# Two left sides of the fast products begin 192 bytes further, and four small tiles get four buffers: a four-layer hybrid trunk

## Chip, cores and metric

One core of one Trainium2 chip runs the whole program. The metric is the device time of one execution in microseconds; a kernel's figure is the median of its runs. The engines are named as in the profile: PE (TensorE matmul), PEld (its weight loads), DVE (VectorE), ACT (ScalarE), POOL (GpSimd), SP (the queue that issues most transfers).

## What is computed

A trunk of four layers over x of 512 rows by 1024 columns, all float32. Each layer adds a mixer's output and then a feed-forward network's output to x:

```python
for layer in range(4):
    h = rmsnorm(x, norm_mix[layer])
    mix = s5_mixer / gla_mixer / diff_attn_mixer / s5_mixer   # layers 0, 1, 2, 3
    x = x + mix
    h = rmsnorm(x, norm_ffn[layer])
    g, u = split(h @ w_gate_up)          # 1024 x 5632
    x = x + (silu(g) * u) @ w_down       # 2816 x 1024
return rmsnorm(x, norm_final)
```

The mixers are a diagonal state-space scan (S5, layers 0 and 3), gated linear attention (GLA, layer 1) and differential attention with a chunk mask (layer 2).

## The kernel before

**Number format.** A float32 factor is split into a high half (rounded to fp32r) and a low half (the rest). ACT writes the high half with a cast, DVE the low half with a subtraction. A product is then three fp32r matmuls: high by high, high by low, low by high. Weights are staged from memory into "wst" or "slot" tiles and split into "whl" tiles, which have five buffers (methods `high` and `low`, lines 366 and 374).

**The feed-forward product in seven products.** The product with `w_gate_up` is done per block of 256 hidden columns, 11 blocks in each layer. In a block the four quarter products of rows and depth are replaced by seven products of sums of quarters, a scheme with seven multiplications in place of eight. Each of the seven takes a left side (256 rows by 512 of depth of the normed input, or a sum of such quarters) and a right side (512 by 256 of the weights, or a sum). The left sides are made once in a layer and are used by all 11 blocks. There are seven:

- "11" and "12" lie in one tile, `sides`, of the activations' room (the pool `hp`, tag `hT`, two buffers). That room also holds the normed activations of the mixers and the tile `halves`, from which all left sides are made. `Sides.room` takes both tiles.
- "1", "2", "4", "3" and "22" are tiles `side...` of the layer's own pool `ffn0` to `ffn3`, taken by `Sides.open`. Two small tiles named `edge` (64 and 192 bytes) stand among these to set where they begin.

One product is `seven_product`, whose matmuls all have line 561: two column halves, four depth tiles and three terms, that is 24 matmuls of 128x128 by 128x256. The right side's piece is the stationary operand, loaded by PEld; the left side's piece, 256 columns of float32, is the moving operand:

```python
mm(o, hl[:, x, k, c], side[:, y, k], start=..., stop=...)
```

The PSUM bank's name tells the products apart in the profile: "one" (bank a, sides), "five" (bank c, side), "six" (a, side), "two" (d, sides), "seven" (a, side), "three" (c, side), "four" (a, side), which is also the order of the third and later blocks. So in a block the first "a" and the "d" read `sides`, the five others a `side` tile. Each layer's first two blocks are instead interleaved step by step by a plan that is written out by hand in `ffn`; it holds the making of the left sides ("total", "high", "low") as well, and the "six" of the first block needs the sum that `add22a`, `highSa` and `lowSa` make of two weight quarters. After each three or four blocks come the matmuls of the down projection (lines 394 to 396, whl as moving operand).

**Where the tiles begin.** Pools lie one behind the other in each partition: constants, x, the activations' room `hp`, weights and staging `wp`, norm tiles `normp`, statistics `small`, and then the pool of the stage at work (`ffn0` and so on). By the sizes of the tiles the two buffers of `hp` begin at bytes 30,656 and 47,040, both 192 past a multiple of 256. The five side tiles begin at 132,736 and further, all 128 past a multiple of 256 (and in layers 0 and 3 three of them 384 past a multiple of 512, all others 128).

**Statistics tiles.** The pool `small` gives each kind eight buffers where nothing else is said, and each buffer takes at least 32 bytes. Four kinds matter here: `ms2` (GLA's `readout`, one for each of eight readouts), `st` (one for each of eight heads of the differential attention), `sums` (one for each of its 32 score steps) and `nm` (two for each score step: the row maximum, written by DVE at line 2261 and read by the exponential on ACT at line 2265). The probabilities `pr` of the score steps have four buffers, two for a step.

**Order of the work.** In GLA and the differential attention the order on PE is the written one, and the framework's planner orders the other engines; in the plan of the feed-forward layers all engines follow the written order; in the later blocks the planner orders all of them. Waits come from the planner.

Of the kernel before, what the change touches and what calls it, by code (L numbers as in the profile page):

```python
# [11 lines left out]
F32 = mybir.dt.float32  # L12
F32R = mybir.dt.float32r
# [8 lines left out]
P = 128  # L22
D = 1024
SEQ = 512
NT = SEQ // P
# [42 lines left out]
class Left:  # L68
# [18 lines left out]
    def room(self):  # L87
        self.hT = [self.tr.hp.tile([P, KT, SEQ], F32R, tag="hT", name=f"hT{z}") for z in range(2)]
# [72 lines left out]
class Sides(Left):  # L161
# [13 lines left out]
    def room(self):  # L175
        F = self.tr.hp.tile([P, 4, 4, 256], F32, tag="hT", name="halves")
        self.whole = F
        self.F = {(0, 0): F[:, 0], (1, 0): F[:, 1], (0, 1): F[:, 2], (1, 1): F[:, 3]}
        two = self.tr.hp.tile([P, 2, 2, 4, 256], F32R, tag="hT", name="sides")
        self.place = {"11": two[:, 0], "12": two[:, 1]}  # L180
        self.heads = []

# [104 lines left out]
class Trunk:  # L287
# [278 lines left out]
    def seven_block(self, fp, slots, left, wgu, b, turn, na):  # L566
# [48 lines left out]
        def room1(room=None):  # L615
            load("1", 0, 1, (0, 0), room)

        def room22(room=None):
            load("22", 1, 1, None, room)
# [93 lines left out]
    def ffn(self, l, left, after=None, turn=False, aside=None, small=None):  # L713
# [7 lines left out]
        with self.tc.tile_pool(name=f"ffn{l}", bufs=1, reuse_waits="tile") as fp:  # L721
# [6 lines left out]
            if glued:  # L728
                lent = room()
# [1123 lines left out]
    def gla(self, l, left):  # L1853
# [5 lines left out]
        with self.tc.tile_pool(name="gla", bufs=1) as p:  # L1859
# [32 lines left out]
            hT = left.hT  # L1892
# [79 lines left out]
            def readout(hf, t):  # L1972
                st, o_h = sts[hf], on[hf]
                oo = row(self.tp("op"))
                ms = self.sp.tile([P, 2], F32, tag="ms2", name="ms")
                for z in range(2):
                    h = 2 * hf + z
                    zs = slice(z * 256, (z + 1) * 256)
                    for c in range(2):
                        ch = 2 * t + c  # L1980
                        nc.tensor.matmul(
                            oo[c * 64 : (c + 1) * 64, zs], qT[:, h, ch * 64 : (ch + 1) * 64], st[z][:, ch],
                            start=True, stop=True,
                        )
                for z in range(2):
                    junk = T("e")
                    nc.scalar.activation(
                        junk[:, :256], oo[:, z * 256 : (z + 1) * 256], AF.Square, scale=1.0 / 16.0,
                        accum_out=ms[:, z : z + 1],
                    )  # L1990
                r_ = self.rsqrt(ms[:], 2, 1e-6)
                for z in range(2):
                    h = 2 * hf + z
                    zs = slice(z * 256, (z + 1) * 256)
                    v.scalar_tensor_tensor(
                        o_h[:, t, zs], oo[:, zs], r_[:, z : z + 1], ng[:, h * 256 : (h + 1) * 256],
                        op0=ALU.mult, op1=ALU.mult,
                    )
# [25 lines left out]
            def core(hf):  # L2024


                def after0():
                    if hf:
                        readout(0, 3)
                    updates(hf, 0)  # L2030

                def after1():
                    readout(hf, 0)
                    updates(hf, 1)

                def after2():
                    readout(hf, 1)
                    updates(hf, 2)

                def after3():  # L2040
                    readout(hf, 2)
                    updates(hf, 3)

                return after0, after1, after2, after3
# [84 lines left out]
    def diff(self, l, left):  # L2129
# [4 lines left out]
        with self.tc.tile_pool(name="diff", bufs=1) as p:  # L2134
# [6 lines left out]
            hT, r = left.hT, left.r  # L2141
# [83 lines left out]
            def prepare(j):  # L2225


                room, bufs, tag = (self.wp, 5, "whl") if j == 1 else (p, 1, "hl")
                hl = room.tile([P, 2, 2, SEQ], F32R, tag=tag, name="hl", bufs=bufs)
                src = qks[j // 4][:, :, j % 4]  # L2230
                nc.scalar.copy(hl[:, 0], src)
                v.tensor_tensor(hl[:, 1], src, hl[:, 0].bitcast(F32), op=ALU.subtract)
                qs = p.tile([P, 2, SEQ], F32R, tag="qs", name="qs", bufs=2)
                ks = self.wp.tile([P, 2, 2, SEQ], F32R, tag="whl", name="ks", bufs=5)
                for m in range(2):
                    rows = slice(m * 64, (m + 1) * 64)
                    for z in range(2):
                        to = slice(z * 64, (z + 1) * 64)
                        self.nc.gpsimd.dma_start(qs[to, m], hl[rows, z, 0])
                        self.nc.gpsimd.dma_start(ks[to, m], hl[rows, :, 1])  # L2240
                ready[j] = qs, ks
                st = self.sp.tile([P, 2, NT], F32, tag="st", name="st")
                o_s = p.tile([P, NT, P], F32, tag="o_s", name="o_s", bufs=2)
                kept[j] = st, o_s

# [2 lines left out]
            def scores(i):  # L2248
                j, t = divmod(i, NT)
                ts = slice(t * P, (t + 1) * P)  # L2250
                qs, ks = ready[j]
                st = kept[j][0]
                pr, sums = [], self.sp.tile([P, 4], F32, tag="sums", name="sums")
                ss = [self.sbank("s"), self.sbank("s")]
                for m in range(2):
                    for z in range(2):
                        nc.tensor.matmul(ss[m][:], qs[:, m, ts], ks[:, m, z], start=z == 0, stop=z == 1)  # L2257
                for m in range(2):
                    e = T("pr", 4)
                    nm = self.sp.tile([P, 1], F32, tag="nm", name="nm")  # L2260
                    v.tensor_tensor_reduce(  # L2261
                        e[:], ss[m][:], mask[:, t], -0.125, 3e38, op0=ALU.add, op1=ALU.min, accum_out=nm[:]
                    )
                    sum_ = st[:, 0, t : t + 1] if m == 0 else sums[:, 1:2]
                    nc.scalar.activation(e[:], e[:], AF.Exp, scale=-1.0, bias=nm[:], accum_out=sum_)  # L2265
                    pr.append(e)
                v.reciprocal(sums[:, 2:3], sums[:, 1:2])
                v.tensor_scalar(
                    sums[:, 3:4], st[:, 0, t : t + 1], sums[:, 2:3], self.neglam[:], op0=ALU.mult, op1=ALU.mult
                )  # L2270
                a = pr[0]
                v.scalar_tensor_tensor(a[:], pr[1][:], sums[:, 3:4], pr[0][:], op0=ALU.mult, op1=ALU.add)
                soft[i] = a
# [52 lines left out]
            run(units, 8)  # L2326
            rest()
            prepare(0)
            run(units)

# [17 lines left out]
            done, w1 = {}, []  # L2348
            run(units, 2)
            scores(0)  # L2350
            run(units, 6)
            scores(1)
            run(units, 2)
            for i in range(32):
                j, t = divmod(i, NT)
                if i == 15:
                    run(units)
                    rest()
                src, n = (units, (3, 3)) if i < 15 else (last, (1, 1))
                if i in (15, 28, 31):  # L2360
                    n = (0, 0)
                elif i == 29:
                    n = (0, 2)
                aT = turned(i)
                if t == 0 and j < 7:
                    prepare(j + 1)
                if i < 30:
                    scores(i + 2)
                if i in done:
                    done.pop(i)()  # L2370
                run(src, n[0])
                values(i, aT)
                run(src, n[1])
                if i in (16, 31):
                    back(i // 31)
                if i in (26, 29):
                    w1 += [self.wb(wo, kb, 512) for kb in ((0, 2) if i == 26 else (4, 6))]
                if t == 3:
                    done[i + (2 if j in (6, 7) else 3)] = normalised(j)
# [96 lines left out]
```

## Time and profile before

| | |
|---|---|
| median of three runs | 2313.63 us (2310.96 to 2320.4) |
| the profiled execution | 2315.56 us, of which the span from first to last instruction is 2313.8 |
| mean granted PE clock | 0.987 |
| busy: PE, DVE, ACT, POOL | 2223.6, 1570.6, 1120.3, 280.8 us |
| transfers | 317.83 MB, mean 137 GB/s |
| feed-forward layers (seven products and down projections) | about 243 to 587, 832 to 1139, 1455 to 1764, 1962 to 2268 us |

How to read it: busy time of PE is counted from the start of a matmul to its modelled end, and matmuls overlap, so 24 matmuls of some 280 ns each follow each other in under 3 us. The chain of waits lists, in order of time, the pieces of work that the end of the program waited for: start, length, engine, bank or tile, line and count. In the groups of instructions "out<-in" gives tile names without buffer numbers, and the figure behind the bar is the sum of busy time, then the mean duration.

### The profile page before, as it was taken

How to read it: one execution, taken by the hardware profiler on the slowest of the kernel's cores; microseconds unless marked ns; L12 is line 12 of the kernel's file. 1: busy time of each engine (PE TensorE's matmuls, PEld its weight loads, DVE VectorE, ACT ScalarE, POOL GpSimd, SP SyncE). 2: the span in 40 equal slices, each digit the busy share in tenths (PEclk: the TensorE clock that was granted, in tenths of full speed). 3: DMA queues.
4: the chain of work that ended last, by engine and by line, in shares of the span. 5: the costliest groups of instructions: out<-in, count | busy, mean ns of one | idle time of the engine just before them, and what ended most of it. 6: DMA issues, size and time to landing. Idle time of an engine off the chain costs nothing. (4 is left out here: it accounts for less than half of the span.)

```text
span 2313.8 us, 37222 instructions
## 1 busy us (share of the span) xinstructions
PE 2223.6 (96%) x14847; PEld 1970.8 (85%) x14847; DVE 1570.6 (68%) x2430; ACT 1120.3 (48%) x1865; POOL 280.8 (12%) x386
## 2 busy tenths in 40 slices
PE   5889999999999999999999999999999899999997
PEld 3778979898877799998987787999999788989996
DVE  7873887776624468777744675876766864967674
ACT  5624645454452456555535675744534224635342
POOL 1000141513000011101002131110000100101000
PEclk8999999999999999999999999999999999999999
DMA  4246667664322357666336465886641546766531
GB/s 86 40 112 182 141 165 181 156 176 117 112 73 78 124 134 197 182 164 174 99 116 146 92 143 149 208 225 151 157 109 46 141 142 163 181 166 165 157 79 64
DMA packets 295320, 317.83 MB, mean 137 GB/s; under 512 B 72206, under 2 KB 235338, under 8 KB 294891
## 3 DMA queue, kind: packets, MB, share of 16 engines
q1 hardware_dynamic: 232906, 234.23, 34.0%
q0 software_dynamic: 62240, 81.22, 19.0%
q8 instruction: 117, 1.92, 0.3%
q14 instruction: 57, 0.46, 0.1%
HBM read 283.54 MB, written 16.65 MB: 130 GB/s over the span
## 5 line engine op out<-in xcount | busy, mean ns | idle before, releaser
L374 DVE TENSOR_TENSOR whl<-wst,whl 128x1024 fp32r<-128x1024 f32 x272 | 331.6, 1224 | 256.2 <-ACT whl L366 255.6
L366 ACT CAST whl<-wst 128x1024 fp32r<-128x1024 f32 x272 | 283.9, 1050 | 314.5 <-PE acc L396 223.7
L561 PE MATMUL a<-side,whl 128*128 128x256 f32 x3168 | 385.6, 278 | 6.1 <-ACT r L633 4.3
L561 PEld LDWEIGHTS a<-side,whl 128*128 128x128 f32 x3168 | 373.3, 189 | 7.8 <-ACT r L633 5.1
L394 PE MATMUL acc<-whl,act 128*128 128x512 f32 x704 | 278.3, 396 | 0.9 <-DVE x L544 0.9
L395 PE MATMUL acc<-whl,act 128*128 128x512 f32 x704 | 274.7, 390 | 0.0
L396 PE MATMUL acc<-whl,act 128*128 128x512 f32 x704 | 274.7, 390 | 0.0
L561 PE MATMUL c<-side,whl 128*128 128x256 f32 x2112 | 254.1, 277 | 1.2 <-DVE whl L374 1.2
L561 PEld LDWEIGHTS c<-side,whl 128*128 128x128 f32 x2112 | 246.7, 188 | 1.8 <-DVE whl L374 1.8
L374 DVE TENSOR_TENSOR whl<-slot,whl 128x1024 fp32r<-128x1024 f32 x107 | 130.5, 1223 | 69.6 <-ACT whl L366 69.6
L394 PEld LDWEIGHTS acc<-whl,act 128*128 128x128 f32 x704 | 132.1, 188 | 31.3 <-issue 2.3
L396 PEld LDWEIGHTS acc<-whl,act 128*128 128x128 f32 x704 | 132.2, 188 | 28.1
L395 PEld LDWEIGHTS acc<-whl,act 128*128 128x128 f32 x704 | 132.2, 188 | 25.6
L366 ACT CAST whl<-slot 128x1024 fp32r<-128x1024 f32 x107 | 112.3, 1054 | 81.9 <-PE acc L396 35.1
L394 PE MATMUL acc<-whl,hT 128*128 128x512 f32 x352 | 143.3, 407 | 2.3 <-DVE ro L2203 1.5
L395 PE MATMUL acc<-whl,hT 128*128 128x512 f32 x352 | 138.4, 393 | 0.9 <-DVE whl L374 0.9
L396 PE MATMUL acc<-whl,hT 128*128 128x512 f32 x352 | 138.4, 393 | 0.0
L561 PE MATMUL d<-sides,whl 128*128 128x256 f32 x1056 | 133.7, 283 | 3.2 <-ACT whl L366 3.2
L561 PE MATMUL a<-sides,whl 128*128 128x256 f32 x1056 | 134.4, 283 | 0.0
L561 PEld LDWEIGHTS d<-sides,whl 128*128 128x128 f32 x1056 | 129.0, 191 | 4.0 <-ACT whl L366 4.0
L561 PEld LDWEIGHTS a<-sides,whl 128*128 128x128 f32 x1056 | 129.7, 191 | 1.1
L700 ACT CAST act<-r 128x512 fp32r<-128x512 f32 (+1 forms) x110 | 66.2, 644 | 113.3 <-DVE r L679 105.2
(452 smaller groups left out, 3897.8 us busy)
## 6 DMA issues: line engine op xcount, KB each, us to landing
wst<-in_ffn_w_gate_up_dram SPq DMA_DIRECT2D x88, 512.0 KB, 4.7
wst<-in_ffn_w_down_dram SPq DMA_DIRECT2D x88, 512.0 KB, 4.2
slot<-in_ffn_w_gate_up_dram SPq DMA_DIRECT2D x71, 512.0 KB, 6.2
wst<-in_ffn_w_gate_up_dram POOLq DMA_DIRECT2D x44, 512.0 KB, 6.1
halves<-in_ffn_w_gate_up_dram SPq DMA_DIRECT2D x43, 512.0 KB, 5.8
wst<-in_s_w_glu_dram SPq DMA_DIRECT2D x32, 512.0 KB, 4.8
wst<-in_gla_w_in_dram SPq DMA_DIRECT2D x24, 512.0 KB, 3.8
wst<-in_diff_w_qkv_dram SPq DMA_DIRECT2D x24, 512.0 KB, 3.7
```

Of the source, the lines that this page charges most:

```text
L366: self.last["high"] = self.nc.scalar.copy(hl[:, 0], w[:])
L374: self.last["low"] = self.nc.vector.tensor_tensor(hl[:, 1], w[:], hl[:, 0].bitcast(F32), op=ALU.subtract)
L394: mm(out, lh, rh, start=first, stop=False)
L395: mm(out, lh, rl, start=False, stop=False)
L396: self.last["mm"] = mm(out, ll, rh, start=False, stop=last)
L561: mm(o, hl[:, x, k, c], side[:, y, k], start=first and not (j or k or n), stop=k == 3 and n == 2, skip_group_check=True,)
L700: self.last["act high"] = nc.scalar.copy(dst[:, 0, j], src[:, j])
```

## The change

The tile of "11" and "12" becomes a tile of 4160 float32 per partition (16,640 bytes) of which 4096 are used, from the 48th on, that is 192 bytes further. With it each of the two buffers of the activations' room becomes 256 bytes larger, for all tiles that share the tag. The second buffer then begins 256 bytes further (47,296), the pools behind it 512. The two possible places of the sides are 30,848 and 47,488, 128 past a multiple of 256.

The kinds `ms2`, `st`, `sums` and `nm` get four buffers in place of eight, 16 buffers of 32 bytes fewer, 512 bytes. The pools of the stages then begin where they did.

```diff
         F = self.tr.hp.tile([P, 4, 4, 256], F32, tag="hT", name="halves")
...
-        two = self.tr.hp.tile([P, 2, 2, 4, 256], F32R, tag="hT", name="sides")
+        two = self.tr.hp.tile([P, 4160], F32R, tag="hT", name="sides")
+        two = two[:, 48:4144].rearrange("p (s z k n) -> p s z k n", s=2, z=2, k=4)
         self.place = {"11": two[:, 0], "12": two[:, 1]}
...
-                ms = self.sp.tile([P, 2], F32, tag="ms2", name="ms")
+                ms = self.sp.tile([P, 2], F32, tag="ms2", name="ms", bufs=4)
...
-                st = self.sp.tile([P, 2, NT], F32, tag="st", name="st")
+                st = self.sp.tile([P, 2, NT], F32, tag="st", name="st", bufs=4)
...
-                pr, sums = [], self.sp.tile([P, 4], F32, tag="sums", name="sums")
+                pr, sums = [], self.sp.tile([P, 4], F32, tag="sums", name="sums", bufs=4)
...
-                    nm = self.sp.tile([P, 1], F32, tag="nm", name="nm")
+                    nm = self.sp.tile([P, 1], F32, tag="nm", name="nm", bufs=4)
```

## The prediction

> **What bounds the kernel now.** I read the page first, then the busy time by stretches for the four feed-forward layers, then the chain of waits through one of them, then the tiles' own rows.
>
> ```profile
> PE 2223.6 (96%) x14847; PEld 1970.8 (85%) x14847; DVE 1570.6 (68%) x2430; ACT 1120.3 (48%) x1865; POOL 280.8 (12%) x386
> ...
> L561 PE MATMUL a<-side,whl 128*128 128x256 f32 x3168 | 385.6, 278 | 6.1 <-ACT r L633 4.3
> ...
> L561 PE MATMUL c<-side,whl 128*128 128x256 f32 x2112 | 254.1, 277 | 1.2 <-DVE whl L374 1.2
> ...
> L561 PE MATMUL d<-sides,whl 128*128 128x256 f32 x1056 | 133.7, 283 | 3.2 <-ACT whl L366 3.2
> ...
> L561 PE MATMUL a<-sides,whl 128*128 128x256 f32 x1056 | 134.4, 283 | 0.0
> ```
>
> The same line, the same shape, the same right side (whl): a matmul whose moving operand is one of the five "side" tiles takes 277 to 278 ns, and one whose moving operand lies in the "sides" tile of the activations' room takes 283. Nothing of this is clock or luck, as the spread shows (minimum/median/maximum):
>
> ```profile
> L561 PE MATMUL a<-sides,whl x1056: 274/283/387, 243.1 to 2251.2; 128*128 128x256 f32 x176
> L561 PE MATMUL d<-sides,whl x1056: 274/283/388, 249.4 to 2259.5; 128*128 128x256 f32 x176
> ...
> L561 PE MATMUL a<-side,whl x3168: 276/276/580, 260.6 to 2267.7; 128*128 128x256 f32 x198
> L561 PE MATMUL c<-side,whl x2112: 276/276/387, 255.1 to 2265.0; 128*128 128x256 f32 x192
> ```
>
> A duration here covers a pipeline's depth; what counts is start to start. The chain of waits (start, length, what) gives it, in layer 2's steady blocks:
>
> ```profile
> 1584.60 2.87 PE a L561 x24
> 1587.47 2.74 PE c L561 x24
> 1590.21 2.72 PE a L561 x24
> 1592.93 2.86 PE d L561 x24
> 1595.79 2.74 PE a L561 x24
> 1598.53 2.72 PE c L561 x24
> ...
> 1612.29 2.86 PE d L561 x24
> ```
>
> The first "a" of a block (product "one") and the "d" (product "two") read sides; they take 2.86 to 2.87 us for 24 matmuls (119 ns each). A product on a side tile takes 2.72 (113 ns), but 2.74 when it follows a sides product. From one "d" to the next is 1612.29 - 1592.93 = 19.36 us: seven products, no gap, TensorE alone on the chain. And it is so nearly everywhere in the feed-forward layers:
>
> ```profile
> 243.00:587.00 344.00, 341.30 (x2746) 309.68 (x2745) 266.73 (x409) 174.91 (x292) 98.76 (x148) 1.00 0.59 151
> 832.00:1139.00 307.00, 303.87 (x2251) 287.39 (x2250) 243.67 (x364) 171.63 (x244) 33.83 (x35) 1.00 0.60 157
> 1455.00:1764.00 309.00, 305.84 (x2251) 289.43 (x2250) 231.05 (x267) 154.44 (x207) 28.21 (x24) 0.99 0.64 162
> 1962.00:2268.00 306.00, 303.56 (x2251) 287.75 (x2250) 219.83 (x244) 145.70 (x187) 24.24 (x19) 1.00 0.56 143
> ```
>
> Columns: stretch, its length, then busy PE, PEld, DVE, ACT, POOL. Of each layer's 306 to 344 us TensorE is idle 2.4 to 3.2.
>
> **The change, part by part.**
>
> *The sides tile begins 192 bytes further.* By the allocation of the kernel, the five side tiles begin 128 bytes past a multiple of 256 in all layers (in layers 0 and 3 three of them 384 past a multiple of 512), the sides tile 192 past. The change puts it at 128. The trace shows no other difference between the two kinds than this and the room they lie in, so I take the side tiles' price: a block's seven products would take 7 x 2.72 = 19.04 us in place of 19.36, that is 0.32 per block and 0.16 per sides product (0.14 its own, 0.02 the follower's). Two in each of 11 blocks in 4 layers are 88 products, 14.1 us in all. Bounds from the rows for one product: 0 (no change of rate) and 0.16; a better rate than 2.72 no row shows.
>
> Not all of it arrives. At the start of each layer two blocks are interleaved by a written plan, and there VectorE sets the pace (stretches from the start of that to the third block in layers 0 and 3, and layer 2's steady blocks for contrast; VectorE is the third busy figure):
>
> ```profile
> 248.00:291.00 43.00, 41.71 (x357) 41.10 (x356) 39.63 (x48) 27.39 (x36) 7.62 (x9) 1.00 0.55 126
> ...
> 1967.60:2010.50 42.90, 41.51 (x356) 40.99 (x354) 39.63 (x48) 27.29 (x36) 6.25 (x5) 1.00 0.71 179
> 1584.40:1661.90 77.50, 77.50 (x674) 77.46 (x674) 61.10 (x72) 42.88 (x58) 7.69 (x6) 1.00 0.69 171
> ```
>
> 39.63 of 43 us is 92%, against 61.10 of 77.50, 79%. Where TensorE meets that pace, in layer 0 (DVE's and PE's timelines; start, length):
>
> ```profile
> 259.57 1.22 DVE L374 TENSOR_TENSOR whl<-lent,whl 128x1024 fp32r<-128x1024 f32 x1 [0.53 <-ACT whl L366]
> ...
> 260.60 3.03 PE L561 MATMUL a<-side,whl 128*128 128x256 f32 x24
> ...
> 287.33 2.78 PE L561 MATMUL c<-side,whl 128*128 128x256 f32 x22 [0.40 <-DVE whl L374]
> 291.23 0.50 PE L561 MATMUL a<-side,whl 128*128 128x256 f32 x2 [1.11 <-ACT r L633]
> 292.66 0.39 PE L561 MATMUL d<-sides,whl 128*128 128x256 f32 x1 [0.93 <-ACT whl L366]
> ```
>
> Product "six" of the first block starts at 260.60 with its low right half done at 259.57 + 1.22 = 260.79: there is no slack. The four sides products before it (one and two of both blocks) would bring TensorE there 0.64 us sooner, to wait for the same VectorE result; I count them at nothing. The 43 us between go at VectorE's pace, and the third block's "one" is followed by waits of 0.40, 1.11 and 0.93 for ACT and VectorE: its 0.16 is lost too. Five of 22 are absorbed per layer. The third block's "two" and all later ones run without a wait: 17 per layer.
>
> In layer 2 more is lost, since there the chain leaves TensorE for a transfer:
>
> ```profile
> 1509.96 2.63 PE d L561 x22
> ...
> 1513.66 10.13 DMA wst<-in_ffn_w_gate_up_dram
> ...
> 1532.29 3.09 PE a L561 x24
> ```
>
> The "two" at 1509.96 still counts, the fourth block's two sides products (between 1513.66 and 1532.29) are waited away behind that load. So 3 x 17 + 15 = 66 products x 0.16 = 10.6 us.
>
> Wait and clock: TensorE's clock drops after those waits, in some layers.
>
> ```profile
> 293.58:297.00 3.42, 3.42 (x19) 3.42 (x17) 3.42 (x4) 1.44 (x2) 0.00 (x0) 0.50 0.02 5
> 880.68:884.09 3.41, 2.48 (x21) 2.29 (x20) 3.41 (x5) 3.41 (x5) 0.00 (x0) 1.00 1.23 192
> 1505.32:1508.73 3.41, 2.89 (x13) 2.90 (x14) 3.41 (x6) 2.79 (x5) 1.02 (x1) 0.50 1.11 335
> 2010.49:2013.90 3.41, 2.34 (x17) 2.14 (x18) 3.41 (x5) 3.41 (x6) 0.80 (x1) 1.00 0.45 74
> ```
>
> The figure before the last two is the granted clock: 0.50 for 3.41 us in layers 0 and 2, 1.00 at the same place in 1 and 3. One costs at most 3.41 x 0.5 = 1.7 us. The change lengthens the idle time there by 0.16 in some 2.5, so the two may become one, three or none: 3.4 us to either side, taken as no change. The Trainium skill (TensorE: Matmul & The Clock Gate, "What's actually happening") calls the window a free-running one of 3413 ns; the rows agree in length, and in that equal places differ.
>
> *Room behind it moves.* The activations' buffers grow by 256 bytes each, so weights, staging and norm tiles lie 512 further, the second activations' buffer 256 further; each keeps its place within 256. No instruction, transfer or queue entry is added or moved. Cost nothing; its upper bound is the rival below.
>
> *Four buffers in place of eight* for ms2, st, sums, nm. This frees 16 x 32 = 512 bytes, so the layers' pools start where they did. Sixteen more tiles reuse a buffer (four of each kind) and may need a semaphore entry each; the chain shows such entries as pieces of this size:
>
> ```profile
> 1994.30 0.04 issue
> ...
> L2265 ACT ACTIVATE pr<-pr,nm x64: 705/722/732, 1249.9 to 1418.8; 128x512 f32<-128x512 f32 x64
> L2265 ACT ACTIVATION_READ_ACCUMULATOR pr<-pr,nm x64: 184/187/200, 1250.5 to 1419.4; 128x1 f32 x64
> ```
>
> 16 x 0.04 = 0.6 us at most, nothing at least. I take nothing: nm is last read by the exponential (0.72 us) of its step, four nm back is two steps back, and the "pr" tiles, four of them and two to a step, already make each step wait for the same step's later subtraction. sums is four steps back, st four heads, ms2 four readouts.
>
> **Sum.** The profiled execution took 2315.56 us (span 2313.8), 1.9 over the median 2313.63. 2315.56 - 10.6 = 2305.0 for a profiled one; 2313.63 - 10.6 = 2303.0 for the median, 0.46% down.
>
> **The rivals.**
>
> *The start within 256 bytes isn't what costs; the room is.* Every matmul of this shape with a side operand lies behind byte 132,000, every sides one below 64,000: no row separates the two. Then sides stays at 283 ns and the time at 2313.6. For it: nothing but that gap in the evidence. Against it: nothing in the rows ties a rate to a room. The Trainium skill has no address in the price of a matmul (TensorE: Matmul & The Clock Gate, "Wait — 56ns, not 53.3ns?": start to start is the column count by 2.4 GHz and some 2.5 ns), and SBUF — State Buffer, "Operand start alignment", asks only for multiples of the element's size, without times; by both, 2313.6 as well. The trace differs from the first, with 113 and 119 ns where it gives 109. Chance 0.17.
>
> *Nothing is absorbed.* VectorE's chain in the plan starts from TensorE's transposes, and could move up with them: 88 x 0.16 = 14.1, 2299.5. Against it: the 92%. Chance 0.15.
>
> *The smaller buffers bind in the attention's 32 score steps.* If each step waited for the exponential two steps on, up to 0.72 + 0.19 = 0.91 us, 32 steps would cost 29 us: 2313.6 - 10.6 + 29 = 2332. It decides from 10.6 / 32 = 0.33 us per step on. Against it: the pr tiles' order above. Chance 0.04.
>
> *The weights' move by 512 bytes counts.* By the loops of the code 4320 matmuls of 512 columns read whl as moving operand; if a start cost them the 6 ns that sides loses to side, 26 us: 2329. Against it, the side tiles' busy time alone in layers 1 and 3 (PE first):
>
> ```profile
> 832.00:1139.00 307.00, 154.31 (x1320) 152.14 (x1320) 6.19 (x6) 5.34 (x6) 1.00 0.60 157
> ...
> 1962.00:2268.00 306.00, 154.44 (x1320) 152.15 (x1320) 6.19 (x6) 5.33 (x6) 1.00 0.56 143
> ```
>
> In layer 3 three of the five begin 256 further within 512 than in layer 1, at the same rate. Chance 0.04.
>
> **How the numbers follow.** Main forecast 0.60, its own range 2298 to 2308 (two clock windows and the runs' scatter either way). The range 2297 to 2314 takes in the 14.1 case below and half of the 0 case above; the other half and the 0.08 slower are left out. Half a percent, 11.6 us, is about what a measurement of this kernel tells from no change, and 10.6 lies just short of it: of the main case 0.4 falls beyond, of the 14.1 case 0.8, of the 0 case few. Faster 0.37, same 0.55, slower 0.08.
>
> **What the profile after would show.** sides rows at 276/276 with products of 2.72; a steady block of 19.04; six of the first block waiting some 0.6 us longer for whl, the third block's "six" about 0.2; layers shorter by 2.7, 2.7, 2.4, 2.7; score steps and 512-column matmuls as before. The prediction is wrong if sides keeps 283 ns, if a layer's first 48 us shrink, or if GLA or attention grow.

## The result: 0.35% slower

The changed kernel takes 2325.15 us (median of 20 runs, 2318.24 to 2331.53) against 2316.6 for the kernel before (20 runs beside them): a ratio of 1.0035, 95% interval 1.0026 to 1.0044. Forecast were 2303.0 and a gain of 10.6; it became a loss of 8.55.

The profiled execution took 2319.07 us, with a span of 2317.2. First the groups of the page after; the line of all feed-forward products is now 562:

```profile
L562 PE MATMUL a<-side,whl 128*128 128x256 f32 x3168 | 392.9, 281 | 7.1 <-ACT r L634 4.5
...
L562 PE MATMUL c<-side,whl 128*128 128x256 f32 x2112 | 259.5, 279 | 1.8 <-DVE whl L375 1.8
...
L562 PE MATMUL d<-sides,whl 128*128 128x256 f32 x1056 | 130.4, 280 | 3.2 <-ACT whl L367 3.2
L562 PE MATMUL a<-sides,whl 128*128 128x256 f32 x1056 | 131.4, 281 | 0.0
```

The two kinds of left sides are alike now, as they should be: 280 to 281 ns. But they did not meet at 277 to 278. The sides products became faster by 2 to 3 ns and the side products, whose tiles did not move, slower by 2 to 3, and there are five of these to two of those.

The chain of waits through layer 2's steady blocks shows what a block looks like after:

```profile
1582.03 2.83 PE a L562 x24
1584.85 2.83 PE c L562 x24
...
1590.51 2.83 PE d L562 x24
1593.33 2.83 PE a L562 x24
...
1598.99 5.65 PE a L562 x48
```

Every product takes 2.83 us, 117.8 ns per matmul, where a sides product took 2.86 and a side product 2.72. The last row holds "four" and the next block's "one", so a block lasts from 1582.03 to 1598.99 + 5.65 / 2 = 1601.82, 19.79 us in place of 19.36. In another stretch of the same execution, PE's timeline (start, and a length that includes the last matmul's tail) shows the block that was forecast:

```profile
465.08 2.88 PE L562 MATMUL a<-sides,whl 128*128 128x256 f32 x24
467.80 2.88 PE L562 MATMUL c<-side,whl 128*128 128x256 f32 x24
...
473.24 2.88 PE L562 MATMUL d<-sides,whl 128*128 128x256 f32 x24
...
484.12 2.88 PE L562 MATMUL a<-sides,whl 128*128 128x256 f32 x24
```

From one "one" to the next 484.12 - 465.08 = 19.04 us, each product 2.72. So the same program, with all left sides at 128, has two rates: 113.3 and 117.8 ns per matmul. A stretch is the run of blocks between two down projections. Behind the interleaved starts there are nine steady stretches with 29 blocks; counted by starts in the trace, each runs at one rate from end to end, eight at 117.8 and one (three blocks, the second stretch of layer 0) at 113.3. In these nine that makes 26 x (19.79 - 19.36) - 3 x (19.36 - 19.04) = 10.2 us over before. The blocks ahead of each layer's first down projection give some 2.4 back. In layers 1 and 3 the products behind the third block's waits ran at 113.3 as well, which saves 0.6 in each. In layer 0 it is 1.3, where the granted clock was 0.50 for 3.41 us before and 1.00 at the same place after; in layer 2 nothing is saved. So from first to last product the four layers took 1263.0 us before and 1270.8 after, by the starts in the two traces: 7.8 more, against a loss of 8.55 in the medians. The profiled pair as a whole differs by 3.5 only, because in that execution the first product came 3.1 us earlier (240.0 against 243.1) and the stages between the four layers took 1.2 less.

One such stretch of layer 1, start to end, in the windows of before, after, and the best of the experiments (the second figure is its length):

```profile
958.90:1036.20 77.30, 77.30 (x672) 77.28 (x671) 58.22 (x66) 40.59 (x51) 7.73 (x6) 1.00 0.71 174
...
953.10:1032.10 79.00, 79.00 (x672) 78.96 (x672) 58.31 (x66) 40.27 (x51) 7.73 (x6) 1.00 0.70 171
...
957.30:1033.40 76.10, 76.10 (x674) 76.10 (x673) 57.34 (x65) 40.15 (x51) 7.73 (x6) 1.00 0.70 175
```

Granted clock 1.00 and TensorE without a gap in all three: neither a wait nor the clock makes the difference between them.

### The profile page after: what moved, and what is told of

Its sections match the earlier page's. It is cut to its first block, busy times and chain, and to the rows that moved or that the text cites. A ratio compares the mean times of both kernels' runs of the same rounds, so it can differ in the third digit from the quotient of the medians.

```text
span 2317.2 us, 37223 instructions
## 1 busy us (share of the span) xinstructions
PE 2225.4 (96%) x14847; PEld 1974.4 (85%) x14847; DVE 1570.5 (68%) x2430; ACT 1119.5 (48%) x1865; POOL 280.9 (12%) x386
## 5 line engine op out<-in xcount | busy, mean ns | idle before, releaser
L562 PE MATMUL a<-side,whl 128*128 128x256 f32 x3168 | 392.9, 281 | 7.1 <-ACT r L634 4.5
L562 PEld LDWEIGHTS a<-side,whl 128*128 128x128 f32 x3168 | 379.9, 189 | 9.1 <-ACT r L634 5.3
L562 PE MATMUL c<-side,whl 128*128 128x256 f32 x2112 | 259.5, 279 | 1.8 <-DVE whl L375 1.8
L562 PEld LDWEIGHTS c<-side,whl 128*128 128x128 f32 x2112 | 251.5, 189 | 2.6 <-DVE whl L375 2.6
```

Of the source, the lines that this page charges most:

```text
L562: mm(o, hl[:, x, k, c], side[:, y, k], start=first and not (j or k or n), stop=k == 3 and n == 2, skip_group_check=True,)
```

## The experiments

The theory after the result (cadence): a stream of products whose moving operand begins at 128 can run at 113 or at 118 ns and keeps the rate with which it began; a product at 192 runs at 119 to 120 and leaves 113 behind it. In the kernel before two products of each block at 192 kept the other five at 113. The rivals: the weights' move by 512 bytes slows the products, or the four statistics buffers bring waits. Ratios are to the kernel before, with runs on the same chip.

**Everything but the 192 bytes** (against the kernel after):

```diff
-        two = two[:, 48:4144].rearrange("p (s z k n) -> p s z k n", s=2, z=2, k=4)
-        self.place = {"11": two[:, 0], "12": two[:, 1]}
+        at = lambda n: two[:, n : n + 2048].rearrange("p (z k n) -> p z k n", z=2, k=4)
+        self.place = {"11": at(0), "12": at(2048)}
```

> The whole change but for the 192 bytes: the enlarged room, the moved pools and the four buffers stay, both sides halves begin 192 past a multiple of 256 again. Cadence theory (a stream of products at 128 can run at 113 or at 118 ns per matmul and keeps what it has; a product at 192 runs at 119 and leaves 113 behind it): sides products 2.86 us, side products 2.72 again, time of before, 2316.6 within 3. Move theory (the weights lie 512 bytes further, and that slows side products to 118 at times): side products stay a mixture of 2.72 and 2.83, sides at 2.86, 5280 matmuls x 2.6 ns = 13.5 us over before, about 2330. Buffer theory (four statistics buffers add waits in GLA or attention): about 2325, with GLA and attention longer.

Both begin 192 past a multiple of 256 here. Measured: 2315.51 us (11 runs) against 2314.45, 0.9997 (0.9988 to 1.0006). Its chain:

```profile
1585.42 2.87 PE a L562 x24
1588.30 2.74 PE c L562 x24
1591.04 2.72 PE a L562 x24
1593.76 2.86 PE d L562 x24
```

That is the block of before to 0.01 us. Room, moved pools and buffers together cost nothing that this interval of some 2 us either way can show; the 192 bytes make the loss. Move and buffer theory fall. The attention bears it out (the row maxima of the 64 half steps, first and last start, before and after):

```profile
L2261 DVE DVE_READ_ACCUMULATOR2_ANT nm<- x64: 82/83/89, 1249.7 to 1418.0; 128x1 f32 x64
```

```profile
L2262 DVE DVE_READ_ACCUMULATOR2_ANT nm<- x64: 78/84/85, 1247.3 to 1415.4; 128x1 f32 x64
```

168.3 and 168.1 us.

**Half the change.** In `one192` only "12" moves, in `two192` only "11" (`at` as above):

```diff
+        self.place = {"11": at(0), "12": at(2096)}
```

```diff
+        self.place = {"11": at(48), "12": at(2112)}
```

The first is `one192`, with "11" at 192 and "12" at 128 past a multiple of 256; the second is `two192`, the other way round.

> Of the change only half: '12' (product two) at 128, '11' (product one) back at 192. Cadence theory: one product of a block resets the other six, 'one' 2.86, all others 2.72 to 2.74, a block of 19.2 us in place of 19.36; some 35 products 'two' outside the plans gain 0.16 each, 5.6 us: 2311. Move theory: side products mixed as in the kernel after, about 2327. If address alone sets a rate: halfway between before and after, 2321.

> The other half: '11' at 128, '12' at 192. Cadence theory: the three products ahead of a stretch's first 'two' may run at 118 (3 x 0.11 us in up to 11 stretches, 3.6 us at most), all behind it at 113: 2311 to 2315. Move theory: about 2327. Address alone: 2321.

Measured: one192 2311.96 us, 0.9989 (0.9980 to 0.9999); two192 2312.5, 0.9989 (0.9980 to 0.9997). Half the change is faster than before by 0.11%, with intervals that end just below 1, and the whole is slower by 0.35%. If each address had a rate of its own, the two halves would add up to the whole; they add up to a gain of 0.22%. Such a rule is out. The chain of one192:

```profile
1574.93 2.87 PE a L562 x24
1577.80 2.74 PE c L562 x24
1580.54 2.72 PE a L562 x24
1583.26 2.72 PE d L562 x24
```

One product at 2.87, and behind it products at 2.72 to 2.74, "two" among them. And two192, where a stretch begins with products at 128:

```profile
1583.08 2.83 PE a L562 x24
1585.90 2.83 PE c L562 x24
1588.73 2.83 PE a L562 x24
1591.56 2.87 PE d L562 x24
1594.43 2.74 PE a L562 x24
1597.17 2.72 PE c L562 x24
```

This is the theory in six rows: three products at 118 until the first product at 192 comes, and 113 from there on. Eight of the nine steady stretches begin so. The ninth begins at 113 at once, and it is again the second of layer 0, the one that was fast in the kernel after.

**All seven left sides at 192** (the edges in the layers' pools moved):

> All seven left sides at 192 past a multiple of 256, the rest as after. Cadence theory and any theory in which the start matters: every product 2.86 to 2.88, 5280 matmuls 6 ns longer than at 113, 30 us less what the plans hide: 2340 to 2346. If the start does not matter and only the mixture of places does: 2325 or below.

Measured: 2345.61 us, 1.0137 (1.0122 to 1.0153). Its chain:

```profile
1601.85 2.88 PE c L562 x24
1604.73 2.88 PE a L562 x24
```

120 ns for all, in the plans too. The start matters, and the first rival of the prediction (the room and not the start) falls: the same side tiles in the same pool went from 113 to 120 by 64 bytes, and with 128 the sides tile reaches 113 in its old room.

**Other starts.** All seven at 0, at 64 and at 160 past a multiple of 256 (the tiles behind them stay where they are; for the first two the kind `rs` gets four buffers for room). This is the edit of `all64` around `Sides.open`:

```diff
+            self.edge(fp, 64)
             left.open(fp, ("1", "2") if glued else ("1", "2", "4", "3", "22"))
-            self.edge(fp, 64)
+            self.edge(fp, 128)
...
-                self.edge(fp, 192)
+                self.edge(fp, 128)
                 left.open(fp, ("4", "3", "22"))
```

`all0` has no edge ahead, then 192 and 64; `all160` has 32, 32 and 224. "11" and "12" begin at floats 32 and 2080 of their tile in `all64`, 16 and 2064 in `all0`, 56 and 2104 in `all160`.

> All seven left sides at a multiple of 256 (the edges in the layers' pools moved, the act tiles where they were, and four buffers for one more kind of statistics tile to make room). If the start counts modulo 128: the same two rates as at 128, 113 and 118, mostly 118, 2325 within 6. If it counts modulo 256, this place has a rate of its own: with 16 cycles fewer, 107 to 109 ns, 2295 or less.

> All seven at 64 past a multiple of 256, otherwise as all0. If the start counts modulo 128: as at 192, 120 ns throughout, 2345 within 4. If modulo 256: a rate of its own, anywhere from 113 to 127 ns, 2305 to 2370.

> All seven left sides at 160 past a multiple of 256, 32 past a multiple of 128. If a matmul's price grows with the distance of its start from a multiple of 128 (or with the line pieces touched): between 113 and 120, with 8 cycles per 32 bytes 116.7 ns, 2330 within 6. If only two classes exist, 0 and not 0 modulo 128: 120 ns, 2346.

Measured: all0 2332.4 us, 1.0079 (1.0065 to 1.0093); all64 2345.94, 1.0139 (1.0124 to 1.0154); all160 2331.2, 1.0075 (1.0053 to 1.0096). A product "two" of each chain, in this order:

```profile
1602.51 2.83 PE d L562 x24
```

```profile
1610.71 2.88 PE d L562 x24
```

```profile
1600.21 2.84 PE d L562 x24
```

At 0 that is the slow rate of 128, 117.8 ns, and all nine steady stretches of all0 ran at it. So did its plans, which run at 113.3 in the kernel after, and its time is above the 2325 forecast for a period of 128 bytes. But behind the third block's waits in layer 3 its chain has the fast rate, for the rest of that block and the whole fourth:

```profile
2041.08 2.72 PE c L562 x24
2046.52 2.72 PE d L562 x24
```

So a start at 0 has both rates, 113.3 and 117.8, as one at 128. At 64 eight of the nine steady stretches ran at 120, as at 192; the plans, the blocks behind them and the first steady stretch of layer 0 ran at 2.85, 118.7 ns, which no product of all192 did. From layer 3:

```profile
2059.59 2.85 PE d L562 x24
```

So 0 goes with 128, and 64 with 192 but for that second rate, which leaves open whether the period is 128 bytes or longer. At 160 the price lies between, 118.3 ns. No start gave less than 113. The right sides' pieces, which are loaded as weights, begin at 192 in every run by the allocation; whether the start counts by itself or against theirs was not tried.

**What sets the rate.** The kernel after, with idle matmuls ahead of the first "one" of a stretch. Their moving operand is the block's weights (at 192), or in `idle128` the left side itself (at 128); "one" overwrites what they leave:

```diff
+            for k in range(ahead):          # 3, 12 or 1; only where a stretch begins
+                nc.tensor.matmul(bank[:, :256], hl[:, 0, k % 4, :P], hl[:, 0, k % 4], start=True, stop=True, ...)
+                # idle128: moving operand A[side][:, 0, k % 4]
```

> The kernel after, with three idle matmuls ahead of the first 'one' of each stretch of blocks (behind the plans and behind each down projection). Their moving operand is the block's own weights, which begin at 192; their result is overwritten. Cadence theory, if three at 192 are enough to set the stream: all products of the steady stretches at 113.3, stretches of 76.6 us where before had 77.3 and after 79.0; before less 10.6 plus 13 x 0.36 = 4.7, about 2309. If three are not enough: after plus up to 4.7, 2325 to 2330.

> The same with twelve idle matmuls, half a product. Cadence theory: side and sides rows at 113 in all steady stretches; the time carries 13 x 1.44 = 18.7 us less what waits hide, 2318 to 2325. If the stream's rate is set by something else than the matmuls ahead: mostly 118 as after, 2335 to 2345.

> As reset3, three idle matmuls ahead of each stretch, but with a moving operand that begins at 128 (the left side itself) in place of 192. If a matmul at 192 is what sets the stream: no effect, mostly 118 in the steady stretches as in the kernel after, 2325 plus up to 4.7. If any work ahead of the stretch does it: 113 throughout the steady stretches, 2316 as reset3.

> One idle matmul at 192 in place of three. If one is enough to set the stream: 113 in all steady stretches of 76.1 us, 3 us less idle work than reset3, 2309 to 2314. If it takes more than one: stretches of 79.0 us, about 2326.

> reset3 without the idle matmuls behind the plans, so ahead of ten stretches. Steady stretches at 113, 76.1 us, as reset3; the third blocks as in the kernel after. If the 4.2 us wait that reset3 had in the second layer's down projection was a matter of where one transfer landed: without it 2308 to 2312. If it comes with a shorter stretch every time: 2314 to 2317.

Measured: reset3 2316.48 us, 1.0001 (0.9986 to 1.0015); reset12 2315.97, 1.0005 (0.9992 to 1.0018); idle128 2329.8, 1.0063 (1.0045 to 1.0082); reset1 2326.29, 1.0046 (1.0031 to 1.0061); reset3b 2311.43, 0.9985 (0.9975 to 0.9995). PE's timeline of reset3 where a stretch begins, and its chain:

```profile
1586.16 0.52 PE L629 MATMUL a<-whl 128*128 128x256 f32 x3
...
1586.51 2.90 PE L562 MATMUL a<-sides,whl 128*128 128x256 f32 x24
```

```profile
1589.41 2.72 PE c L562 x24
...
1594.85 2.72 PE d L562 x24
```

Against it the first "one" behind the idle matmuls in the chains of reset1 and of idle128:

```profile
1589.27 2.83 PE a L562 x24
```

```profile
1597.57 2.83 PE a L562 x24
```

Behind three matmuls at 192, 0.35 us, a stretch of 76.1 us keeps the fast rate; all nine steady stretches of reset3 and reset12 ran at 113. Three at 128 do nothing (one of nine fast, once more the second of layer 0), and one at 192 is too little (two of nine, the first two of layer 0). In reset3b, which has them ahead of nine stretches, eight were fast; the first of layer 0 ran at 117.8 although three matmuls at 192 stood ahead of it. So of three idle matmuls it is the start that makes the difference, not that there is work ahead, and it works nearly always.

It is not the start alone. The down projection's matmuls, which stand ahead of the steady stretches in every kernel, have 512 columns, and by the allocation their moving operand, a weights tile, begins at 192 too. The chain of the kernel after shows 27 of them ahead of a stretch:

```profile
1575.91 0.23 PE acc L395
...
1581.80 0.23 PE acc L397
1582.03 2.83 PE a L562 x24
```

They follow each other in (1582.03 - 1575.91) / 27 = 226.7 ns, twice 113.3, so 512 columns at 192 show none of the cost that 256 columns have there; and the stretch behind them runs at 117.8. Seven of the nine stretches stand right behind such a run without a gap, and all seven were slow in the kernel after. The one that was fast has a break shortly ahead, 16 small matmuls with three of the down projection's behind them:

```profile
444.60 0.68 PE L1246 MATMUL xps<-ident,halves 64*64 64x64 f32 x16
```

Whether that break decides was not tried; the first stretch of layer 0, which has 16 small matmuls right ahead of it, was slow.

reset3 came out 7 us above its forecast of 2309, though its steady stretches were as fast as forecast, and reset12 below its range. Part of the 7 us is in the second down projection of layer 1: the waits of PE and of ACT there (waiter, releaser; total, times, longest), and PE's in reset3b:

```profile
PE acc L395 <- DVE x L545: 4.2, 1, 4.2
```

```profile
ACT cssp L1274 <- DMA cs<-cssp: 3.1, 2, 2.6
```

```profile
PE acc L395 <- DVE x L545: 0.6, 1, 0.6
```

ACT waited for a spill transfer, VectorE waited for ACT, and the accumulation behind it could not be drained. Around the end of that wait and behind it the granted clock was 0.50 for 6.8 us (1057.32 to 1064.13), and behind the plans of layers 1 and 3 for 3.4 us each; in reset3b it was 1.00 at these three places and 0.50 for 3.4 us behind the plan of layer 2. In reset3b, with as short a stretch ahead of it, the wait was 0.6. So it does not come with every short stretch; how often it comes, one profile for each kernel does not tell.

reset3b has the lowest ratio of this study, 0.15% under before, and one192 with no added matmul is within its interval.

## Why the prediction was wrong

**What bounds the kernel** stood: TensorE, without a gap, in the feed-forward layers.

**The term that failed** is the price of a side product: "I take the side tiles' price", 2.72, with 0 and 0.16 per product as its bounds. 2.72 was not the price of a start at 128 but the faster of two, and the side products had it because a sides product at 192 ran ahead of them in every block. The change took away what kept it. "Nothing of this is clock or luck, as the spread shows" was read from minimum and median, which could not show it, as all side products stood in the same company. The bound below zero was missing: 5 x (2.83 - 2.72) lost against 2 x (2.86 - 2.83) and the followers' 2 x 0.02 gained is 0.45 per block, against 19.79 - 19.36 = 0.43 measured.

The trace of before had the second rate. Right behind the last row that the prediction quotes for layer 2's transfer (1532.29), the chain of before reads:

```profile
1535.38 2.83 PE c L561 x24
1538.21 2.83 PE a L561 x24
```

Two side products at 2.83, at the one place where the stream starts anew behind a wait on a side product and ends before the next sides product. An unexplained 0.11 in rows of the same kind said that a side product had a second price.

**What is absorbed at the start of a layer** stood in layer 0, from whose rows it was read. PE's timeline of layer 0 after, whose first product starts at 240.0:

```profile
256.96 0.39 PE L562 MATMUL a<-side,whl 128*128 128x256 f32 x2
257.73 2.86 PE L562 MATMUL a<-side,whl 128*128 128x256 f32 x22 [0.38 <-DVE whl L375]
...
284.29 2.78 PE L562 MATMUL c<-side,whl 128*128 128x256 f32 x22 [0.54 <-DVE whl L375]
288.19 0.50 PE L562 MATMUL a<-side,whl 128*128 128x256 f32 x2 [1.12 <-ACT r L634]
```

"Six" of the first block starts 16.96 us after the layer's first product, 0.5 sooner than before, and now waits 0.38 for the same VectorE result. The third block's "six" starts 288.19 - 240.0 = 48.2 after it, against 48.1: nothing arrived, as forecast.

**Moved pools and four buffers at nothing** stood, by both192. **The rivals**: the one with the room fell by all192, the weights' move and the binding buffers by both192. The one in which nothing is absorbed used the same 0.16 per product and fell with it. The outcome was slower, but by none of the mechanisms named for that. Of the clock windows at 0.50 behind the plans the profile before has two and the one after one, which is within the 3.4 us that the prediction left for them; their share in the medians cannot be told from single profiles.

**The page that was weighed**: the Trainium skill (TensorE: Matmul & The Clock Gate, "Wait — 56ns, not 53.3ns?") gives a warm matmul its columns by 2.4 GHz and some 2.5 ns; an estimate from that is 109.2 ns for 256 columns. These runs have 113.3, 117.8, 118.3, 118.7 and 120 by start and by company, at a granted clock of 1.00; the measurement decides, and no stream here came down to the estimate.

## What to carry to other kernels

A duration measured in a mixture is not the price of one kind of instruction: before taking it for others, look for rows where that kind stands alone, or behind something else, and explain each row of the same kind that is off. When an edit makes instructions alike, ask what the unlike ones did for their neighbours; undoing half of the edit tells. Where a stream without gaps runs at two rates, a few idle instructions at its start can pay: three of them, 0.35 us, turned a stretch of 79.0 us into one of 76.1.

## What the hardware showed that was not expected

A back-to-back stream of 128x256 fp32r matmuls with a weight load each has rates that depend on where the moving operand begins: 120 ns at 192 past a multiple of 256 bytes, 118.7 or 120 at 64, 118.3 at 160, and at 0 and 128 either 113.3 or 117.8 for as long as nothing interrupts it (76 us and more at 128). Matmuls of 512 columns at 192 took 226.7 ns, twice 113.3. Three matmuls of 256 columns at 192 ahead brought the stream at 128 to 113.3 in 17 of 18 steady stretches of reset3 and reset3b, where three at 128 left it at one of nine, as in the kernel after. Whether a stretch at 128 starts fast or slow does not look like chance: the same one of nine steady stretches started fast in the kernel after, in two192, in idle128 and in reset1. What in the work ahead of it decides that, and what inside the engine holds the rate, stays open.
